# Moving one 32-byte tile so that the matmul operands of both layers start at 0 modulo 256 bytes

## The chip, the cores and the metric

The kernel runs as one program on one core of a Trainium2 chip. The metric is the device time of one execution in microseconds (us), lower is better. Engines are named as in the profile: PE is the matrix engine (PEld its loads of the stationary operand), DVE, ACT and POOL are the vector, scalar and GpSimd engines, SP issues most of the DMAs.

## The reference: what is computed

Two layers of a diffusion transformer on 256 image tokens and 256 context tokens, model width 2048, branch width 4096, all in float32. Cut to what matters:

```python
# layer 0: Fourier mixing, for x and for the context
u, z = split(h @ w_in)                        # h: 256 x 2048, w_in: 2048 x 8192
f = real(fft2(u, groups of 256)) ; f = einsum(f, w_mix)
x = x + gate * ((f * silu(z)) @ w_out[0])     # 4096 x 2048
# layer 1: attention, 64 query heads of 64, 8 key/value heads, window 128 plus the context
q, k, v, z = split(h @ w_in)                  # 2048 x 9216
o = softmax_with_sink(q k^T + mask) v
x = x + gate * ((o * silu(z)) @ w_out[1])
return rmsnorm(x, final_g)
```

In front of each layer stands `h = rmsnorm(x) * (1 + scale) + shift`, where shift, scale and gate come from a small product of the conditioning vector with 2048 x 6144 weights.

## The kernel before, in words

Every large product is done three times in a 32-bit format (`float32r`): both operands are split into a rounded high part and the rest, and PE adds high x high, high x low and low x high. The helper `mm3` (its three `PE.matmul` calls are lines 78 to 80 of the profile) does this. In `PE.matmul(o, stationary, moving)` the second argument is the stationary operand, which PEld loads (128 columns), and the third one is the moving operand, which streams through (up to 512 columns). While a matmul streams, PEld loads the stationary operand of the next.

```python
def mm3(o, wh, wl, xh, xl, start, stop):
    PE.matmul(o, wh, xh, start=start, stop=False)
    PE.matmul(o, wh, xl, start=False, stop=False)
    return PE.matmul(o, wl, xh, start=False, stop=stop).ins
```

Weights come in by DMA into `raw` tiles (128 x 2048, 3 buffers), and `half_split` cuts each into two halves of 1024 columns: ACT rounds one into `wh` (line 65), DVE subtracts to get `wl` (line 66). Activations lie in `act` tiles (128 x 512) in layer 0.

The stages, in the order of the program:
- Opening and Fourier part (to about 322 us): conditioning, a discrete Fourier transform over tokens, the product with the first half of `w_in`. Stationary operands are slices of 127 columns of the tiles `wmh`, `wml`, `wph`, `wpl`; the moving one is an `act` tile, 256 or 260 columns at a time.
- z and output products of layer 0 (322 to 1028 us): the stationary operand is 128 columns of `wh` or `wl`, the moving one a whole `act` tile of 512 columns. These are the groups `ps<-act,wh` and `ps<-act,wl`, 1024 matmuls for each of the lines 78 to 80. A group's name gives what is written, then the moving and then the stationary operand.
- k and v products of layer 1 (1028 to 1122 us): here the roles are swapped. The stationary operand is 128 columns of `h1` or `h1c` (the layer's input, high part in columns 0 to 255 and rest in 256 to 511), the moving one 512 columns of `wh` or `wl`: groups `ps<-wh,h`, `ps<-wl,h`, `ps<-wh,h1c` and so on, 384 matmuls.
- q products (768 matmuls of the same form with `h1`), z products (`ps<-h,wh` of line 1119 with 512 moving columns of `h1`, `ps<-h,wl` of line 1121 with 256) and attention, interleaved by hand (1122 to 1640 us). A loop over 64 heads does `stage_s` (scores: four matmuls `kkh` and `kkl` against `qa` or `qb`, lines 1155 and 1156, then maximum and exponential on DVE and ACT), one filler unit of a projection, `stage_o` of two heads earlier (eight float16 matmuls of lines 1190 and 1191) and another filler unit. A filler unit of q or of the output product is 12 matmuls. The first ten units run ahead of the loop.
- Output product of layer 1 (partly as filler, then 1640 to 1800 us): the moving operand is again `wh` or `wl`; the stationary one, 128 columns of `yh[k]`, lies for k = 0 to 15 in the buffers of the `h1` pool, for k = 16 to 23 in `act` tiles, for k = 24 to 31 in the pool `fin`.

The tile that the change moves is `dsc` (128 x 8 float32, 32 bytes in each partition): eight columns of scale factors, which `emit_y` reads as a per-partition scalar. It was allocated from the pool `h1`, ahead of that pool's 16 large buffers.

Pools are laid out one behind the other in each partition's memory, so the size of one sets the start of the next. `const` (the constants) comes first, then `raw`, `ws` (with `wh`, `wl`, `xh`), `act`, and behind them the pools of the stages. No scheduler's table and no queue is touched by the change.

Of the kernel before, what the change touches and what calls it, by code (L numbers as in the profile page):

```python
# [10 lines left out]
F32 = mybir.dt.float32  # L11
# [6 lines left out]
P = 128  # L18
# [13 lines left out]
def tile_dit(ctx: ExitStack, tc: tile.TileContext, a: dict, out: bass.AP):  # L32
# [3 lines left out]
    const = ctx.enter_context(tc.tile_pool(name="const", bufs=1))  # L36
# [66 lines left out]
    GP.memset(ones, 1.0)  # L103
    mhalf, pow_end = const.tile([P, 4], F32, name="mhalf"), [None]
    GP.memset(mhalf, -0.5)

    def bcast_rows(r4, dst):
        o = psum()
        for t in range(4):
            PE.matmul(o[:, t * P : (t + 1) * P], r4[:, t : t + 1].broadcast_to([P, P]), ident, start=True, stop=True)  # L110
        S.copy(dst, o)
# [775 lines left out]
    with tc.tile_pool(name="h1", reuse_waits="tile", bufs=16) as h1p:  # L887
        hx1 = []
        v01, vs = [], []
        dsc = h1p.tile([P, 8], F32, name="dsc", bufs=1)  # L890
        kT = []
        with tc.tile_pool(name="kvp", reuse_waits="tile", bufs=2) as kvp:
            hc1 = []
# [561 lines left out]
```

## Time and profile before

| what | value |
|---|---|
| time, median of 3 runs | 1803.8 us |
| the 3 runs | 1804.04, 1803.8, 1799.57 us |
| profiled execution: span of its instructions | 1799.6 us |
| profiled execution: its own time | 1799.6 us, nothing around the span counts; it agrees with the third run |
| PE busy | 1765.1 us, 98% of the span |
| PEld busy | 1478.0 us, 82% |
| DVE busy | 1411.3 us, 78% |
| ACT busy | 898.3 us, 50% |
| DMA | 398.86 MB, mean 222 GB/s |

The profiled execution is thus as quick as the quickest of the three runs, 4.2 us under their median. Two things matter in reading the page. Matmuls are pipelined: the duration of one in a record is longer than the distance from its start to the next one's start, so a chain of matmuls is timed by the distance of starts. And a view that counts the instructions in a stretch also counts those that straddle its ends, which makes a count of matmuls up to two too high.

### The profile page before, as it was taken

The numbers are of one execution on the slowest core, as the hardware profiler recorded it, in microseconds if no ns is written. First come the engines' busy times: TensorE is split into PE (matmuls) and PEld (weight loads), VectorE is DVE, ScalarE is ACT, GpSimd is POOL, SyncE is SP. The second block draws the span as 40 slices with busy tenths as digits, with TensorE's granted clock in tenths as the row PEclk, the third lists the DMA queues.
The fourth block names the chain that finished last, engine by engine and source line by source line (L and its number), as shares of the span: only waits on it lengthen the run. The fifth ranks groups of instructions, "written<-read, shape, count | busy, mean of one in ns | idle before, by whom it ended". The sixth has DMA issues, their size and how long they took to land. (4 is left out here: it accounts for less than half of the span.)

```text
span 1799.6 us, 26039 instructions
## 1 busy us (share of the span) xinstructions
PE 1765.1 (98%) x9449; PEld 1478.0 (82%) x9449; DVE 1411.3 (78%) x2761; ACT 898.3 (50%) x1543; POOL 213.5 (12%) x213
## 2 busy tenths in 40 slices
PE   6999999999999999999999999999999999999998
PEld 4679999888888888888888888878888788887886
DVE  5779888786978888775976563989999899997455
ACT  5545445432222242323322443678887788886343
POOL 0001112100000000000001000332212212233001
PEclk9999999999999999999999999999999999999999
DMA  9998889666666757663558322488888988888553
GB/s 393 417 341 230 236 228 249 230 227 241 239 229 234 260 194 264 245 223 117 189 203 336 120 104 94 168 189 217 213 209 204 211 209 209 211 211 263 192 176 140
DMA packets 205248, 398.86 MB, mean 222 GB/s; under 512 B 152064, under 2 KB 152464, under 8 KB 170048
## 3 DMA queue, kind: packets, MB, share of 16 engines
q1 hardware_dynamic: 181056, 359.19, 61.7%
q0 software_dynamic: 19920, 31.06, 6.7%
q10 hardware_dynamic: 4144, 6.95, 1.2%
q8 instruction: 74, 1.21, 0.3%
q14 instruction: 54, 0.44, 0.1%
HBM read 352.06 MB, written 12.59 MB: 203 GB/s over the span
## 5 line engine op out<-in xcount | busy, mean ns | idle before, releaser
L65 ACT CAST wh<-raw 128x1024 fp32r<-128x1024 f32 x333 | 348.3, 1048 | 532.4 <-PE ps L79 431.6
L66 DVE TENSOR_TENSOR wl<-raw,wh 128x1024 fp32r<-128x1024 f32 x333 | 428.0, 1289 | 219.1 <-ACT wh L65 215.4
L79 PE MATMUL ps<-act,wh 128*128 128x512 f32 x1024 | 398.2, 389 | 0.0
L78 PE MATMUL ps<-act,wh 128*128 128x512 f32 x1024 | 393.7, 389 | 0.0
L80 PE MATMUL ps<-act,wl 128*128 128x512 f32 x1024 | 392.8, 389 | 0.0
L80 PEld LDWEIGHTS ps<-act,wl 128*128 128x128 f32 x1024 | 192.2, 188 | 39.9
L79 PEld LDWEIGHTS ps<-act,wh 128*128 128x128 f32 x1024 | 192.2, 188 | 39.8
L78 PEld LDWEIGHTS ps<-act,wh 128*128 128x128 f32 x1024 | 192.2, 188 | 39.7
L1119 PE MATMUL ps<-h,wh 128*128 128x512 f32 x512 | 184.8, 396 | 0.0
L686 DVE CUSTOM_DVE_ANT_0 raw<-raw,cb 128x512 f32<-128x512 f32 x256 | 172.7, 689 | 12.7 <-DMA raw<-in_adw 8.9
L686 DVE CUSTOM_DVE_ANT_0 junk<-raw,cb 128x512 f32<-128x512 f32 x192 | 132.1, 688 | 31.0 <-DMA raw<-in_adw 20.4
L1121 PE MATMUL ps<-h,wl 128*128 128x256 f32 x512 | 138.6, 281 | 0.0
L79 PE MATMUL ps<-wl,h 128*128 128x512 f32 x320 | 126.9, 397 | 0.3 <-DVE wl L66 0.3
L80 PE MATMUL ps<-wh,h 128*128 128x512 f32 x320 | 125.3, 395 | 0.0
L78 PE MATMUL ps<-wh,h 128*128 128x512 f32 x320 | 124.0, 402 | 0.0
L1173 DVE SCALAR_TENSOR_TENSOR f<-p,sm,f 128x512 f16<-128x512 f32 x128 | 105.6, 844 | 11.1 <-ACT f L1172 10.9
L1119 PEld LDWEIGHTS ps<-h,wh 128*128 128x128 f32 x512 | 96.2, 188 | 18.9
L1160 ACT ACTIVATE p<-ps,mx 128x512 f32<-128x512 f32 x128 | 88.0, 689 | 36.9 <-DVE mx L1157 30.8
L1172 ACT ACTIVATE f<-p,sm 128x512 f16<-128x512 f32 x128 | 87.6, 717 | 33.6 <-DMA ft<-f 15.5
L1121 PEld LDWEIGHTS ps<-h,wl 128*128 128x128 f32 x512 | 96.6, 189 | 2.8
L1157 DVE CUSTOM_DVE_ANT_0 ps<-ps,mask,nsink 128x512 f32<-128x512 f32 x128 | 93.5, 750 | 0.9 <-PE ps L1156 0.7
L79 PE MATMUL ps<-wl,ys 128*128 128x512 f32 (+1 forms) x192 | 75.2, 392 | 0.0
(339 smaller groups left out, 3379.3 us busy)
## 6 DMA issues: line engine op xcount, KB each, us to landing
raw<-in_wz SPq DMA_DIRECT2D x64, 1024.0 KB, 5.4
raw<-in_adw SPq DMA_DIRECT2D x64, 1024.0 KB, 5.2
raw<-in_awp SPq DMA_DIRECT2D x32, 1024.0 KB, 13.0
raw<-in_wo SPq DMA_DIRECT2D x32, 1024.0 KB, 5.5
raw<-in_wq SPq DMA_DIRECT2D x32, 1024.0 KB, 5.3
raw<-in_wu SPq DMA_DIRECT2D x32, 1016.0 KB, 6.1
raw<-in_wo1b SPq DMA_DIRECT2D x16, 1024.0 KB, 4.9
act<-in_xT POOLq DMA_DIRECT2D x32, 256.0 KB, 6.0
```

The costliest lines, as they stand in the source:

```text
L65: last_cast[0] = S.copy(h, src).ins
L66: last_sub[0] = eng.tensor_tensor(l, src, h.bitcast(F32), op=ALU.subtract).ins
L78: PE.matmul(o, wh, xh, start=start, stop=False)
L79: PE.matmul(o, wh, xl, start=False, stop=False)
L80: return PE.matmul(o, wl, xh, start=False, stop=stop).ins
L686: V.tensor_tensor_reduce(junk if s == 0 and i < 3 else wf, wf, cb[:, s, kq * 512 : kq * 512 + 512], 1.0, 0.0, ALU.mult, ALU.add, acc[:, i, ...
L1119: PE.matmul(o[0], wh[:, q], hx1[k], start=k == 0, stop=k == KT - 1)
L1121: PE.matmul(o[0][:, 0:N], wl[:, q], hx1[k][:, 0:N], start=False, stop=False)
L1157: V.tensor_tensor_reduce(o, o, mask[:, tb, :], -0.125, nsink[:, i : i + 1], ALU.add, ALU.min, mx[:, tb : tb + 1])
L1160: S.activation(pt[tb], so[tb], AF.Exp, bias=mx[:, tb : tb + 1], scale=-1.0, accum_out=sm[:, tb : tb + 1])
L1172: S.activation(f[:, 0:512], pt[tb], AF.Copy, scale=sm[:, tb : tb + 1])
L1173: V.scalar_tensor_tensor(f[:, 512:1024], pt[tb], sm[:, tb : tb + 1], f[:, 0:512], op0=ALU.mult, op1=ALU.subtract)
```

## The change

`dsc` is allocated from `const`, right behind `mhalf`, and no longer from the pool `h1`.

```diff
     mhalf, pow_end = const.tile([P, 4], F32, name="mhalf"), [None]
     GP.memset(mhalf, -0.5)
+    dsc = const.tile([P, 8], F32, name="dsc")
...
     with tc.tile_pool(name="h1", reuse_waits="tile", bufs=16) as h1p:
         hx1 = []
         v01, vs = [], []
-        dsc = h1p.tile([P, 8], F32, name="dsc", bufs=1)
         kT = []
```

`const` grows by 32 bytes, so all that is laid out behind it moves up by 32 bytes, as far as the pool `h1`: that pool loses the 32 bytes in front of its buffers, which therefore stay where they were, and so does everything behind them. Start addresses in a partition, in bytes, from the two built programs:

| tiles | before | after | modulo 256 before | after |
|---|---|---|---|---|
| `raw` | 19680 + n x 8192 | 19712 + n x 8192 | 224 | 0 |
| `wh`, `wl`, `xh`, `xl` | 44256 + n x 4096 | 44288 + n x 4096 | 224 | 0 |
| `act` | 68832 + n x 2048 | 68864 + n x 2048 | 224 | 0 |
| `h1`, `yh` 0 to 15 | 142080 + n x 2048 | the same | 0 | 0 |
| `h1c` | 175360 + n x 2048 | the same | 0 | 0 |
| `kkh`, `kkl`, `qa`, `qb` | from 174848, 178944, 183040, 189184 | the same | 0 | 0 |
| `yh` 24 to 31 (pool `fin`) | 832 modulo 2048 | the same | 64 | 64 |
| `dh`, `dl` (token transform) | 185632, 189728 | the same | 32 | 32 |
| Fourier tiles (`wmh`, `aph`, `pqh`, ...) | various | all 32 higher | various | various |

A slice of a stationary operand (128 columns of float32) is 512 bytes on from the last, so it keeps the remainder; only the Fourier slices of 127 columns run through all multiples of 4.

On all five engines the two programs hold the same instructions in the same order, with the same waits; only addresses differ. Lines behind the new one are numbered one higher, and the same again behind the removed one.

## The prediction

> **What bounds the kernel now.** I read the page first (its busy shares), then the groups of matmuls by line and form, then stretches of the span with their counts, and last single starts in the timeline.
>
> ```profile
> PE 1765.1 (98%) x9449; PEld 1478.0 (82%) x9449; DVE 1411.3 (78%) x2761; ACT 898.3 (50%) x1543; POOL 213.5 (12%) x213
> PEclk9999999999999999999999999999999999999999
> ```
>
> PE is busy for 98% of the span at full granted clock. No clock is to be won, so the time moves only with what one matmul takes or with how long PE stands. The groups show that one shape, 128 stationary columns against 512 moving ones, has two durations (out, then moving and stationary operand; count, then busy us and mean ns of one):
>
> ```profile
> L80 PE MATMUL ps<-act,wl 128*128 128x512 f32 x1024 | 392.8, 389 | 0.0
> L79 PE MATMUL ps<-wl,h 128*128 128x512 f32 x320 | 126.9, 397 | 0.3 <-DVE wl L66 0.3
> L80 PE MATMUL ps<-wh,h1c 128*128 128x512 f32 x64 | 24.7, 396 | 0.0
> L79 PE MATMUL ps<-wl,ys 128*128 128x512 f32 x184 | 73.0, 397 | 0.0
> L79 PE MATMUL ps<-wl,act 128*128 128x512 f32 x56 | 21.8, 390 | 0.0
> ```
>
> Row one is layer 0: both operands at 224 modulo 256 bytes, 389 ns. Rows two to four are layer 1: moving operand at 224, stationary one at 0 (in `ys` partly 64), 396 to 397 ns. Row five is the control inside layer 1: the same moving `wl`, but the stationary operand lies in `act`, at 224 again, and it takes 390 ns. So it isn't the stage; it goes with where the two operands lie to each other. What counts for the time is the distance of starts, which a stretch of back-to-back matmuls gives:
>
> ```profile
> core 0: us, PE busy (x), PEclk, DMA share, GB/s
> 330.00:700.00 370.00, 370.00 (x1635) 1.00 0.63 230
> 1032.00:1117.00 85.00, 85.00 (x365) 1.00 0.30 104
> 1657.00:1701.00 44.00, 44.00 (x190) 1.00 0.54 192
> 1702.00:1723.00 21.00, 21.00 (x94) 1.00 0.58 201
> ```
>
> With two straddlers taken off: 370 / 1633 = 226.6 ns in layer 0; 85 / 363 = 234 and 44 / 188 = 234 ns with the stationary operand at 0. The last two rows are one loop, the output product of layer 1; only at about 1701 us does the stationary operand go from the `h1` buffers to `act`, and 21 us then hold 94, less two 228, less one 226 ns. In the timeline:
>
> ```profile
> 599.81 0.39 PE L79 MATMUL ps<-act,wh 128*128 128x512 f32 x1
> ...
> 600.49 0.39 PE L79 MATMUL ps<-act,wh 128*128 128x512 f32 x1
> ...
> 1278.40 0.39 PE L79 MATMUL ps<-wl,h 128*128 128x512 f32 x1
> ...
> 1279.79 0.40 PE L79 MATMUL ps<-wl,h 128*128 128x512 f32 x1
> ```
>
> Three matmuls in 0.68 us, 226.7 ns each, against six in 1.39 us, 231.7 ns. I take 226.7 and 233.2: the second is the mean of the stretches and of the filler units, and 6.5 ns the difference.
>
> **The change part by part.**
>
> *Layer 0, no term.* All of `wh`, `wl`, `xh`, `act` and the Fourier tiles move by the same 32 bytes, so no pair changes its relation. I take 0 for 3072 matmuls. What speaks for it is that a pair with both at 0 can be seen, the scores of attention:
>
> ```profile
> 1272.17 0.40 PE L78 MATMUL ps<-wh,h 128*128 128x512 f32 x1
> ...
> 1272.87 0.40 PE L1155 MATMUL ps<-kkh,qa 128*128 128x512 f32 x1
> 1273.10 0.39 PE L1156 MATMUL ps<-kkl,qa 128*128 128x512 f32 x1
> 1273.33 0.39 PE L1155 MATMUL ps<-kkh,qa 128*128 128x512 f32 x1
> 1273.55 0.39 PE L1156 MATMUL ps<-kkl,qa 128*128 128x512 f32 x1
> ```
>
> The three q matmuls ahead (224 against 0) take 0.70 us; three scores (0 against 0) take 0.68, as in layer 0. Not every head looks like this, though:
>
> ```profile
> L1155 PE MATMUL ps<-kkh,qa 128*128 128x512 f32 x64 | 25.4, 397 | 0.0
> L1156 PE MATMUL ps<-kkl,qa 128*128 128x512 f32 x64 | 25.0, 391 | 0.0
> ```
>
> By these means (397 and 391, against 389) a pair at 0 costs 2 to 8 ns more, with waits in line 1155. But these chains are four long, and a chain at 224 against 224 starts slowly too:
>
> ```profile
> 1630.76 0.39 PE L79 MATMUL ps<-wl,act 128*128 128x512 f32 x1
> ...
> 1632.61 0.40 PE L79 MATMUL ps<-wl,act 128*128 128x512 f32 x1
> ```
>
> Eight matmuls behind float16 ones take 1.85 us, 231 ns each, before a chain settles. So I read the means of the scores as unsettled chains. The ends for layer 0: a gain or loss of 3 ns each, 9 us both ways, if the settled distance at 0 is another.
>
> *Layer 1 outside attention.* The moving `wh` and `wl` come to 0, against `h1` and `h1c` at 0. By the loops: 384 matmuls of k and v, 120 of q ahead of the heads, and 288 in the last stage (k = 0 to 15, less the 96 that are filler), together 792, at 6.5 ns 5.1 us. PE stands nowhere there that matters, so all of it shortens the span. The 180 with `yh` 24 to 31 go from 224 against 64 to 0 against 64, a relation that no row shows: between minus and plus 6.5 ns, 1.2 us both ways; taken at 0.
>
> *Layer 1 inside attention.* 648 of q and 96 of the output product, in units of 12. A unit behind the scores would follow on a settled chain (6.5 ns); one behind the float16 matmuls has to settle first. From 231 for the first eight and 226.7 then, against 233.2, that is about 2.9 ns. Half and half, 4.7 ns: 3.5 us. The 256 scores themselves then no longer follow on an unsettled chain: 3 ns, 0.8 us (from 391 against 389 and the excess of 397, less its waits). The z products, 512 pairs:
>
> ```profile
> L1119 PE MATMUL ps<-h,wh 128*128 128x512 f32 x512 | 184.8, 396 | 0.0
> L1121 PE MATMUL ps<-h,wl 128*128 128x256 f32 x512 | 138.6, 281 | 0.0
> 1253.64 0.39 PE L1119 MATMUL ps<-h,wh 128*128 128x512 f32 x1
> ```
>
> They go from 0 against 224 to 0 against 0. Mean 396 with waits in it, yet single ones take 0.39, so they are nearer to the fast kind: between minus 2 and plus 6.5 ns; I take 2, 1.0 us. Together 5.3 us of PE time. Not all of it is span:
>
> ```profile
> 1160.00:1640.00 480.00, 473.14 (x2605) 392.07 (x2603) 446.91 (x826) 394.35 (x783) 123.92 (x99) 1.00 0.85 207
> PE ps L1190 <- DMA ft<-f: 4.7, 4, 2.1
> ```
>
> DVE (the third figure) works 447 of these 480 us, 93%. With 5 us less it would be at 94%, so PE stays the longer one; but PE already waits 4.7 us for `ft`, which hangs on DVE and ACT, and that wait is what comes late next. I count three quarters, 4.0 us; the ends are 2 and 5.3.
>
> *The opening.* `raw` is also where the weights land. The first 90 us are full of DMA:
>
> ```profile
> 0.00:90.00 90.00, 73.42 (x557) 51.09 (x558) 55.39 (x150) 48.95 (x82) 3.84 (x13) 1.00 0.99 405
> gbc<-gated POOLq DMA_DIRECT2D x1, 1024.0 KB, 7.4
> raw<-in_wo1b SPq DMA_DIRECT2D x16, 1024.0 KB, 4.9
> ```
>
> A load of the same size that already lands at 0 (`gbc`) is no quicker than one into `raw` at 224 (7.4 against 4.9 us, though on another queue), so I take 0, with 0 to 2 us as ends. The Trainium skill, "DMA: Bandwidth & Descriptors", "How a descriptor splits into AXI transactions", says that a descriptor not starting at a multiple of 256 bytes needs one transaction more; by its figures a row of 8192 bytes would go from 264 to 256 beats, an estimate of 3% of the opening's loads into `raw`. No run here shows that for SBUF writes.
>
> *The moved tile itself.* `dsc` is read as a scalar operand by the same 32 instructions; no instruction, wait or queue entry is added, removed or moved. Zero; what hides it is that DVE isn't on the end-setting path there.
>
> The sum: 5.1 + 4.0 = 9.1 us. From the profiled execution's 1799.6 us that is 1790.5; it lies 4.2 us under the median of the runs, from which it is 1803.8 - 9.1 = 1794.7 us, 0.50% less.
>
> **The rivals.**
>
> *Slower: the stationary operand's own place decides.* All slow rows have it at 0 or 64 and all settled fast ones at 224, so "224 is the good place" fits the long stretches as well. Then layer 0 falls to the slow kind: 3072 x 6.5 = 20.0 us more, layer 1 gains nothing, 1823.8 us. It decides from 9.1 / 3072 = 3.0 ns per matmul of layer 0 on. Against it stand the scores at 1272.87 us, settled with the stationary operand at 0. Chance 0.12.
>
> *No change: the distances don't come from the addresses,* or nothing of the gain reaches the end. Time 1803.8 us. The control rows (390 against 397 in one stage) speak against it, and the tail, where no engine but PE is close. Chance 0.10. The Trainium skill, "TensorE: Matmul & The Clock Gate", "Step-by-step: what each phase is for", is on this side: PE has two independent SBUF read ports, and loading the next weights takes no bandwidth from the running matmul. By it all those chains should have one distance; the trace disagrees (226.6 against 234 ns).
>
> *Faster by the loads too:* the opening's DMA gets quicker by up to 2 us on top, 1792.7 us. Chance 0.04, by the `gbc` row.
>
> **How the numbers follow.** The forecast, relation decides and layer 0 stays, has 0.74; its own range is 1789 to 1800 us: the attention part between 2 and 5.3, the two unknown relations by 1.2 and by 1 to 2, and a spread of runs of about 2 us. 0.3% of this kernel is 5.4 us, about what its measurement can tell from no change; runs here differ by 4.5. Of the forecast's share 0.12 falls within 0.3%, the rest is faster: with the loads 0.66 faster. Within 0.3%: 0.12 + 0.09 of no change + a weak form of the first rival (1 to 4 ns in layer 0) 0.02, so 0.23. Slower 0.11. The range goes from 1787 us (the sum, the upper ends of the attention part and of the loads, and the runs' spread) to 1806 (no change and the runs' spread); the first rival lies outside, as does a gain of 3 ns in layer 0.
>
> **What would show it.** Right: in 1032 to 1117 us about 377 matmuls where 365 stood, groups `ps<-wl,h`, `ps<-wh,h1c` at 389 to 391 ns, layer 0 still at 389 and 1635 in 370 us, `ps<-wl,ys` between 390 and 397 for its part at 64. Wrong: layer 0 at 392 or more (first rival); layer 1 still at 396 (second); or layer 1 at 390 and the stretch of the heads as long as before, with the waits for `ft` grown by as much.

## The result, and the profile after

The changed kernel took 1797.65 us (median of 8 runs, 1796.45 to 1800.93), the kernel before beside it 1803.69 us (8 runs, 1799.57 to 1804.44). The ratio is 0.9973, 95% interval [0.9963, 0.9982]: 6.0 us less by the medians. In a later comparison it was 1797.87 against 1802.33 us, ratio 0.9966 [0.9951, 0.9982]. The profiled execution after has a span of 1795.5 us against 1799.6 before, only 4.1 us less. Every other run here with both figures on record took 1.7 to 1.9 us longer than its span, so the profiled execution of before would stand at about 1801.4 us (an estimate), 2.3 us under its median, and not be the run of 1799.57 us, as the table ahead of the prediction reads it. That of after, 1797.29 us, lies 0.4 under its own median, so the two spans show less of the gain than the medians do.

The page, and then the same four stretches of the span that the prediction showed (us; PE busy us and number of matmuls; granted clock; DMA share; GB/s):

```profile
PE 1760.7 (98%) x9449; PEld 1479.2 (82%) x9449; DVE 1411.9 (79%) x2761; ACT 897.8 (50%) x1543; POOL 211.5 (12%) x213
```

```profile
330.00:700.00 370.00, 370.00 (x1634) 1.00 0.62 230
1032.00:1117.00 85.00, 85.00 (x376) 1.00 0.31 111
1657.00:1701.00 44.00, 44.00 (x196) 1.00 0.55 194
1702.00:1723.00 21.00, 21.00 (x94) 1.00 0.56 191
```

Layer 0 holds 1634 matmuls in 370 us where it held 1635, so it is where it was. The k and v products hold 376 in 85 us instead of 365, the output product 196 in 44 us instead of 190. The fourth row, where the stationary operand lies in `act`, had 94 and has 94. With the straddlers off, 85 / 374 = 227 ns: layer 1 now goes at the pace of layer 0.

The groups by line and form (count, then busy us and mean ns of one):

```profile
L80 PE MATMUL ps<-act,wl 128*128 128x512 f32 x1024 | 392.8, 389 | 0.0
L1119 PE MATMUL ps<-h,wh 128*128 128x512 f32 x512 | 187.4, 403 | 0.0
L1121 PE MATMUL ps<-h,wl 128*128 128x256 f32 x512 | 138.7, 281 | 0.0
L79 PE MATMUL ps<-wl,h 128*128 128x512 f32 x320 | 125.2, 391 | 0.9 <-DVE wl L66 0.9
L79 PE MATMUL ps<-wl,ys 128*128 128x512 f32 x184 | 72.3, 393 | 0.0
L1155 PE MATMUL ps<-kkh,qa 128*128 128x512 f32 x64 | 25.3, 395 | 0.0
L80 PE MATMUL ps<-wh,h1c 128*128 128x512 f32 x64 | 24.2, 389 | 0.0
```

`ps<-wl,h` fell from 397 to 391 and `ps<-wh,h1c` from 396 to 389, as forecast. `ps<-wl,ys`, part of which stays unequal (0 against 64), stopped at 393. One row went the wrong way: the z product of line 1119 rose from 396 to 403 ns.

Where the 4.1 us between the two profiles lie follows from the start times of the same matmul in both traces (us):

| stretch, from one matmul's start to the next one's | before | after | difference |
|---|---|---|---|
| start to first z matmul of layer 0 (opening, Fourier) | 322.3 | 321.1 | -1.2 |
| z and output products of layer 0 | 696.9 | 696.9 | 0.0 |
| row sums to first k, v matmul | 9.3 | 9.3 | 0.0 |
| k and v products | 89.7 | 87.2 | -2.5 |
| q ahead of the heads | 42.0 | 41.0 | -1.0 |
| attention (first score to last `ft,v` matmul) | 480.8 | 483.0 | +2.2 |
| output product after it | 149.3 | 147.6 | -1.7 |

Outside attention 6.4 us came in, in attention 2.2 were lost again; the remaining 0.1 is rounding. About 1.6 of the 2.2 us, by an estimate, is a stretch at half the granted clock that this execution has in attention and that of before has not (shown in the last section). The stretch 1160 to 1640 us (PE, PEld, DVE, ACT, POOL, clock, DMA) and PE's waits there:

```profile
1160.00:1640.00 480.00, 471.10 (x2599) 390.97 (x2598) 443.88 (x818) 391.32 (x778) 123.96 (x102) 1.00 0.86 210
```

```profile
PE ps L1190 <- ACT f L1172: 3.6, 3, 2.2
PE ps L1190 <- DMA ft<-f: 1.7, 3, 0.8
PE ps L1190 <- DVE ft L1183: 1.7, 1, 1.7
PE ps L1182 <- DVE f L1173: 1.1, 1, 1.1
PE ps L79 <- DVE wl L66: 0.9, 3, 0.5
```

The four rows for `f` and `ft` sum to 8.1 us (before 6.7). 1.7 of them is a wait at the end of the heads (`ft` L1183; 0.9 before, behind 1640 us) that comes and goes: it is 1.7 in the kernel below whose gain is undone (`pad_h1`), and 0.9 in one that keeps the gain (`fin_at_0`).

### The profile page after: what moved, and what is told of

Its sections match the earlier page's. It is cut to its first block, busy times and chain, and to the rows that moved or that the text cites. A ratio compares the mean times of both kernels' runs of the same rounds, so it can differ in the third digit from the quotient of the medians.

```text
span 1795.5 us, 26039 instructions
## 1 busy us (share of the span) xinstructions
PE 1760.7 (98%) x9449; PEld 1479.2 (82%) x9449; DVE 1411.9 (79%) x2761; ACT 897.8 (50%) x1543; POOL 211.5 (12%) x213
## 5 line engine op out<-in xcount | busy, mean ns | idle before, releaser
L79 PE MATMUL ps<-act,wh 128*128 128x512 f32 x1024 | 398.2, 389 | 0.0
L78 PE MATMUL ps<-act,wh 128*128 128x512 f32 x1024 | 393.7, 389 | 0.0
L79 PEld LDWEIGHTS ps<-act,wh 128*128 128x128 f32 x1024 | 192.2, 188 | 39.8
L78 PEld LDWEIGHTS ps<-act,wh 128*128 128x128 f32 x1024 | 192.2, 188 | 39.8
L79 PE MATMUL ps<-wl,h 128*128 128x512 f32 x320 | 125.2, 391 | 0.9 <-DVE wl L66 0.9
L78 PE MATMUL ps<-wh,h 128*128 128x512 f32 x320 | 122.4, 397 | 0.0
L79 PE MATMUL ps<-wl,ys 128*128 128x512 f32 (+1 forms) x192 | 74.5, 388 | 0.0
```

## The experiments

Two theories were open after the result. *Relation:* the pace hangs on how the starts of the moving and the stationary operand stand to each other modulo 256 bytes. *Place:* it hangs on the stationary operand's own start; the unchanged layer 0 (224 before, 0 after) already speaks against that. And for the 3.5 us that did not arrive in attention: is PE time there no longer worth anything, or was less of it saved than forecast? Start distances below are means over all undisturbed matmuls of 512 columns that follow another one, from the trace's single starts; a pair is written moving, then stationary start, modulo 256 bytes.

**One pool moved back.** A 32-byte tile ahead of the `h1` pool; the weights stay at 0.

```diff
     with tc.tile_pool(name="h1", reuse_waits="tile", bufs=16) as h1p:
+        pad1 = h1p.tile([P, 8], F32, name="pad1", bufs=1)
+        GP.memset(pad1, 0.0)
```

> The changed kernel with 32 bytes more ahead of the buffers of layer 1's pool, so that wh, wl and act stay at 0 modulo 256 and h1, h1c, kkh, qa go to 32 (yh 24 to 31 to 96). Relation theory (what counts is the distance of the two operands modulo 256, not where they lie): layer 1 is as in the kernel before, projections back at 233 ns (groups wh,h at 395 to 397), z products back at 229.5 ns, 1803 us, 0.998 to 1.002 of the kernel before; layer 0 stays at 226.7. Place theory (a start at 0 modulo 256 is good or bad by itself): z products, whose stationary operand wh stays at 0, stay at 234 ns, and the scores, now both at 32, change.

Measured 1802.76 us (11 runs), ratio to before 0.9998 [0.9988, 1.0009]. The stretches of layer 0 and of k and v, and the group of the z product (its line is 1121 in this kernel):

```profile
330.00:700.00 370.00, 370.00 (x1634) 1.00 0.62 230
1032.00:1117.00 85.00, 85.00 (x366) 1.00 0.30 106
```

```profile
L1121 PE MATMUL ps<-h,wh 128*128 128x512 f32 x512 | 184.7, 396 | 0.0
```

366 matmuls instead of 376: the k and v products are slow again (233.3 ns, 0 against 32). The z product is quick again (396, distance 229.7 at 32 against 0, where it had 0 against 224 before). Moving less stationary start is minus 32 in the one, as it was at 224 against 0, and plus 32 in the other, as it was at 0 against 224: both pace and difference are those of before, though each stationary operand lies somewhere else than it did. The place theory falls. Layer 0, which the edit leaves alone, keeps its 1634.

**The other pool moved.** The same pad between `ws` and `act`: layer 0's moving operands at 32, its weights at 0.

```diff
+    padp = ctx.enter_context(tc.tile_pool(name="pad", bufs=1))
+    pad0 = padp.tile([P, 8], F32, name="pad0")
+    nc.gpsimd.memset(pad0, 0.0)
     actp = ctx.enter_context(tc.tile_pool(name="act", bufs=33))
```

> The changed kernel with 32 bytes more ahead of the pool act: wh and wl stay at 0, act and all of layer 1's tiles go to 32. Relation theory: the 3067 matmuls of layer 0 lose their common start (moving 32 above stationary) and leave 226.7 ns for somewhere between 228 and 234: 4 to 22 us on top of the kernel before, 1808 to 1826 us, with the last stage's part on act tiles slow too; layer 1 as before. Place theory (the stationary operand's own start decides): layer 0's stationary wh stays at 0 as in the changed kernel, 226.7 ns, at most 1804 us.

Measured 1822.4 us (4 runs), ratio 1.0114 [1.0098, 1.0129].

```profile
330.00:700.00 370.00, 370.00 (x1588) 1.00 0.61 221
```

```profile
L83 PE MATMUL ps<-act,wl 128*128 128x512 f32 x1024 | 398.9, 395 | 0.0
```

1588 in place of 1634: 370 / 1586 = 233.3 ns. Layer 0's stage grew from 696.9 to 717.3 us, 20.4 us for 3072 matmuls, 6.6 ns each. A difference of plus 32 (32 against 0) costs in layer 0 what minus 32 (224 against 0) cost in layer 1.

**The z weights elsewhere.** In the z product the 512- and the 256-column matmul alternate. The weights get a column offset (0 as the control, 56, 8 or 32 float32 columns), so that they lie at 0, 224, 32 or 128; six constants of layer 0 move to another pool for the room.

```diff
-        h = wsp.tile([P, 1024], F32R, tag="ws", name="wh")
-        l = wsp.tile([P, 1024], F32R, tag="ws", name="wl")
+        h = wsp.tile([P, 1088], F32R, tag="ws", name="wh")[:, off : off + 1024]
+        l = wsp.tile([P, 1088], F32R, tag="ws", name="wl")[:, off : off + 1024]
...
-                return half_split(raws1[src], i % 2)
+                return half_split(raws1[src], i % 2, 56 if kind == "z" else 0)
```

> Control for the next: buffers of wh and wl are 256 bytes longer each (1088 columns, of which 1024 are used from column 0), and the room comes from moving five small layer-0 constants (1536 bytes) into the pool of layer 0; all starts modulo 256 as in the changed kernel. Both theories: as the changed kernel, 1796 to 1800 us, z products at 234.4 and 117.3 ns.

> As the control, but the z products' wh and wl use columns 56 to 1079, so that as stationary operands they start at 224 modulo 256, as before the change, while k, v, q and output products keep 0 against 0. Both theories: z products back from 234.4 to 229.5 and from 117.3 to 118.1 ns, 2.1 us less of PE's work in the attention stretch. If PE bounds that stretch: 2 us quicker than the control, ratio to it 0.9988, 1795.5 us. If DVE, ACT and the transposes bound it: not quicker, 1797.6 us, and PE's waits for ft and f grow by 2 us.

> The z weights at 32 modulo 256 bytes, their moving operand at 0, a pair that no run has shown in these chains. If the difference of the two starts modulo 256 decides, this is the relation of the slow projections (moving 224, stationary 0, 233.3 ns), seen in the z chains: the product of 512 columns takes more than the 229.3 ns of 0 against 224, and the pair with the 256-column one more than 347.2 ns. If only being alike or not counts, it is 229.3 and 118 ns as at 224.

> The z weights at 128 modulo 256 bytes, half a period from their moving operand. If the difference decides smoothly, the pair of 512 and 256 columns takes between the 347.2 ns of 0 against 224 and the 351.7 ns of 0 against 0, or as at 32. If only being alike or not counts, 347.2 ns.

Groups of line 1119 at 0, 224, 32 and 128, in this order:

```profile
L1119 PE MATMUL ps<-h,wh 128*128 128x512 f32 x512 | 186.5, 401 | 0.0
```

```profile
L1119 PE MATMUL ps<-h,wh 128*128 128x512 f32 x512 | 184.9, 397 | 0.0
```

```profile
L1119 PE MATMUL ps<-h,wh 128*128 128x512 f32 x512 | 186.9, 401 | 0.0
```

```profile
L1119 PE MATMUL ps<-h,wh 128*128 128x512 f32 x512 | 186.2, 399 | 0.0
```

| z weights at (moving at 0) | 512 columns, ns | 256 columns, ns | the pair |
|---|---|---|---|
| 0 | 234.4 | 117.2 | 351.6 |
| 224 | 229.5 | 118.2 | 347.7 |
| 32 | 233.6 | 118.1 | 351.7 |
| 128 | 231.5 | 119.4 | 350.9 |

Of the four, 224 is the best place and 0 with 32 the worst, each by one execution. So the sign and size of the difference count, not only whether it is zero, and this chain wants another difference than the projections. Why it does is open: here a load of the stationary operand (188 to 189 ns by the profile) outlasts the matmul of 256 columns that it runs beside (118 ns), which it doesn't in the other chains (227 ns), but no run tests that. But the time doesn't follow: 1797.18 us at 0 (5 runs, ratio 0.9966 [0.9954, 0.9979]), 1797.33 at 224 (11 runs, 0.9970 [0.9961, 0.9979]); the single executions at 32 and 128 gave 1796.21 and 1799.37. At 224 the z matmuls together took 512 x (351.6 - 347.7) ns = 2.0 us less than at 0, the attention 482.5 us against 481.3. But the 482.5 holds a stretch at half clock of about 1.6 us, and the 481.3 none: that execution has it behind attention. So the two profiles can't tell whether part of the 2.0 us arrived, and the whole times show nothing of it.

**The loads' place alone.** The moved tile goes behind `raw`, so `raw` is at 224 again and every matmul operand stays as changed.

```diff
     rawp = ctx.enter_context(tc.tile_pool(name="raw", bufs=3))
+    padp = ctx.enter_context(tc.tile_pool(name="pad", bufs=1))
...
-    dsc = const.tile([P, 8], F32, name="dsc")
+    dsc = padp.tile([P, 8], F32, name="dsc")
```

> The changed kernel with one difference: the 32-byte tile lies behind the raw buffers instead of in the constants, so the raw buffers, where the weights land, are at 224 modulo 256 bytes again and every matmul operand is where the change put it. If the place where the loads land is worth something, the layer-0 output product starts at about 322.3 us of the span (322.3 before, 321.1 after), the 8192-byte packets of the opening take 313 ns instead of 309, and the whole is about 1.2 us longer than the changed kernel, 1798.8 us. If the 1.2 us came from the Fourier matmuls' own operands, or by chance, the product starts at 321.1 us and the time is that of the changed kernel, 1797.6 us.

The first z matmul of layer 0 in the timeline, before, after and in this kernel (where one line more makes L79 of L78):

```profile
322.28 0.39 PE L78 MATMUL ps<-act,wh 128*128 128x512 f32 x1
```

```profile
321.12 0.39 PE L78 MATMUL ps<-act,wh 128*128 128x512 f32 x1
```

```profile
322.43 0.39 PE L79 MATMUL ps<-act,wh 128*128 128x512 f32 x1
```

The first 90 us, after (first row) and here (second row):

```profile
0.00:90.00 90.00, 74.71 (x566) 52.38 (x570) 55.32 (x150) 49.08 (x83) 3.82 (x13) 1.00 0.99 410
```

```profile
0.00:90.00 90.00, 73.21 (x556) 51.26 (x557) 55.32 (x150) 49.07 (x82) 3.81 (x13) 1.00 0.99 406
```

With `raw` at 224 the opening moves 406 GB/s (405 before) and the stage ends at 322.4 us; at 0 it moves 410 and ends at 321.1. The median packet of 8192 bytes between 30 and 60 us took 313 ns in both kernels with `raw` at 224 and 309 ns in both executions of the changed kernel. All other profiles with `raw` at 0 had this start at 320.6 to 321.1 us, but for one at 321.8 (the kernel with z matmuls added, below), which stays open. So the step belongs to the loads' place. The whole time was 1797.86 us (11 runs, 1794.11 to 1802.69), on another chip than the changed kernel's second comparison; the kernel before took 1800.76 us there. The ratio, 0.9982 [0.9971, 0.9993], lies 1.6 to 2.9 us above the 0.9973 and 0.9966 of the changed kernel, the way that was expected, but the intervals overlap.

**The last stationary buffers.** `yh` 24 to 31 from 64 to 0.

```diff
-            ss = fp.tile([P, 9], F32, name="ss")
+            ss = fp.tile([P, 64], F32, name="ss")
```

> The changed kernel with the tile ahead of the last eight stationary buffers widened from 9 to 64 columns, so these eight lie at 0 modulo 256 bytes instead of 64. If the relation of the two starts decides, the 181 matmuls at 0 against 64 (233.2 ns) fall to about 227, 1.1 us less, all of it behind the attention: about 1796.5 us. If 64 is near enough to 0, or their pace comes from something else, they stay at 233.2 and the time is 1797.6 us.

15 us of the last stretch, after (first row) and here (second row, 5 us earlier as the end is):

```profile
1770.00:1785.00 15.00, 15.00 (x72) 1.00 0.12 43
```

```profile
1765.00:1780.00 15.00, 15.00 (x74) 1.00 0.12 43
```

The 181 matmuls fell from 233.2 to 226.7 ns, and the output product after attention from 147.6 to 146.5 us: minus 64 costs as much as 32 either way. The time was 1793.02 us (5 runs, 1792.14 to 1797.18; before beside it 1800.76), ratio 0.9964 [0.9950, 0.9978]. It is the lowest time here, but on the chip where the kernel before is also quicker, and the ratio is that of the changed kernel (0.9966 and 0.9973) within its interval: the 1.1 us are shown by the stage, not by the whole time. The profiled execution also had the shortest attention of all, 479.3 us, in which this edit changes nothing of the pairs and no stretch at half clock lies.

**Both small edits** (z weights at 224, last buffers at 0):

> Both small edits on the changed kernel: the z weights at 224 modulo 256 bytes against their moving operand at 0 (the quicker place, 2.6 us of TensorE time by the run with that edit alone), and the last eight stationary buffers at 0. If the attention is set by other engines, only the second edit arrives: about 1796.3 us. If both arrive, 1793.9 us.

1796.23 us (11 runs), ratio 0.9976 [0.9967, 0.9985]; output product after attention 146.5 us, attention 481.3. The second edit shows in its stage; of the first nothing can be seen in the time.

**Less and more work in attention.** 64 of the 512 low-part z matmuls left out, and the same 64 done twice.

```diff
-                            else:
+                            elif k % 8 != 3:
                                 PE.matmul(o[0][:, 0:N], wl[:, q], hx1[k][:, 0:N], start=False, stop=False)
```

```diff
                                 PE.matmul(o[0][:, 0:N], wl[:, q], hx1[k][:, 0:N], start=False, stop=False)
+                                if k % 8 == 3:
+                                    PE.matmul(o[0][:, 0:N], wl[:, q], hx1[k][:, 0:N], start=False, stop=False)
```

> The changed kernel without 64 of the 512 low-part z matmuls of 256 columns (each eighth k step), so part of the z product is not computed. At 117.3 ns each that is 7.5 us of TensorE time inside the attention. If TensorE sets the attention's length, the stretch from the first score to the last ft,v matmul falls from 483.0 to 475.5 us and the time to about 1790.1 us. If the transposed tiles ft and with them VectorE and ScalarE set it, the stretch stays within 1 us of 481 to 483, the waits of TensorE for ft and f grow by about 7 us, and the time is 1796 to 1798 us. In between, the share of 7.5 us that arrives is the share that any saving of TensorE time in this stage is worth.

> The changed kernel with 64 low-part z matmuls of 256 columns done a second time (the same eight of each 64 that were left out before), so a part of the z product is added twice. That is 7.5 us more TensorE time inside the attention. Leaving 7.5 us out made that stage 9 us longer, with 11 us more waits for ft. If the stage is a balance of TensorE and of the chain that makes ft, with TensorE the longer one on this side, the stage grows by 7 to 9 us to about 491 us, the waits for ft stay or shrink, and the time is about 1805 us. If the chain for ft sets the length and the run without the matmuls was slower only by the way the waits fell, the added work fills waits: the stage stays within 3 us of 483 and the time is 1797 to 1801 us.

PE's waits in attention, with less (three rows) and with more (three rows):

```profile
PE ps L1190 <- DMA ft<-f: 18.1, 16, 5.4
PE ps L1190 <- ACT f L1172: 2.2, 1, 2.2
...
PE ps L79 <- DVE wl L66: 0.6, 2, 0.4
```

```profile
PE ps L1192 <- DMA ft<-f: 5.2, 6, 2.1
PE ps L1192 <- ACT f L1174: 2.1, 1, 2.1
PE ps L1192 <- DVE ft L1185: 1.2, 2, 0.8
```

With 7.5 us less the attention was 491.9 us long and the time 1804.47 us (11 runs, ratio 1.0022 [1.0013, 1.0031]), longer than with them; with 7.5 us more it was 488.2 and 1801.04 us (12 runs, 0.9987 [0.9974, 0.9999]). Neither was expected as it came. The pair is not the clean test it was meant to be: in both built programs, units around the z products stand in another order than in the changed kernel (in the first, the eight `ft,v` matmuls of one head stand behind a z unit instead of inside it). What they show is that the length of this stage hangs on when `ft` comes, whose waits went to 18 us with PE less busy; two stretches at half clock (last section) lie in that execution's attention as well. How much a pure change of PE's work would be worth they don't show.

**The changed kernel again**, beside the kernel before:

> The changed kernel itself, again, beside the kernel before on the same chip. If its gain is that of the first comparison, it is about 6 us, a ratio of 0.9967 to 0.9975. It also settles what the runs with the raw buffers at 224 and with the last stationary buffers at 0 are to be compared with: if the stage gains of the profiles are real, the changed kernel lies 1 us under the first and 1 us over the second.

1797.87 us (10 runs), ratio 0.9966 [0.9951, 0.9982]: the gain is there again, 4.5 us by the medians. The second part of the expectation can't be read from the medians, since the kernels with `raw` at 224 and with the last buffers at 0 ran on another chip. By the ratios, each to the kernel before on its own chip, the first lies 2.9 us over this one and the second 0.4 us under it, where 1 and 1 were expected; the intervals cover both.

**What the attention made of it.** All kernels here but those with less and more work issue the same matmuls there in the same order. The sums of start distances of the q, output, score and z matmuls, each counted without what it waited, and the stage's length (us):

| operands in attention | sum of those matmuls | attention, each profile | mean |
|---|---|---|---|
| as before (before, and the two with a pad) | 403.4 | 480.8, 483.8, 481.6 | 482.1 |
| as after (five profiles) | 401.7 | 483.0, 482.2, 482.4, 481.3, 479.3 | 481.6 |
| z weights at 224 (two profiles) | 400.2 | 482.5, 481.3 | 481.9 |

3.2 us of matmul time went, and the stage's mean changed by 0.2 to 0.5 us, while single profiles of one group differ by up to 3.7. Part of that spread has a name: a stretch at half clock (last section), about 1.6 us, lies in the attention of the profiles with 481.6, 483.0, 482.2, 482.4 and 482.5 us, and partly in the one with 483.8; none lies in the others. The plus 2.2 us between the two profiles of the result is thus mostly such a stretch, and the rest lies within the spread. How much of the saved matmul time arrives in this stage stays open.

## Why the prediction was right, and where its sum was off

1794.7 us was forecast, and 1797.65 measured, inside the range; the gain has the forecast mechanism and two thirds of its size (6.0 of 9.1 us; in the second comparison half, 4.5). By the ratio it is 0.27%, which falls within 0.3% (forecast chance 0.23), by the medians 0.33%, which falls in faster (0.66): it lies at the edge of the two. That the total came so near owes 1.2 us to the opening, which the sum had at nothing. By steps:

- *Layer 0, no term:* right. 696.9 us before and after, 226.7 ns both at 224 and at 0. With that row the rival (the stationary operand's own place) fell, and again in the first experiment.
- *Layer 1 outside attention, 5.1 us:* right. The three stages gave 2.5 + 1.0 + 1.7 = 5.2 us. (The trace has 161 q matmuls ahead of the first score where the sum counted 120; that moves 0.3 us from the next step to this one.) The 180 (181 in the trace) with `yh` 24 to 31 were taken at no change, and 0 against 64 had 233.2 ns, as 224 against 64 had 234.1: right within 0.2 us.
- *Layer 1 inside attention, 4.0 us:* this is the step that failed. Of its 5.3 us of PE time the q and output units gave 3.2 (3.5 forecast, though by its own figures a unit behind float16 matmuls gains 3.6 ns a matmul and not 2.9, which makes 3.8), the scores 0.4 (0.8), and the z products, forecast to gain 1.0, lost 2.0, some 4 ns a pair, outside the ends that were given (minus 2 to plus 6.5). The step took 0 against 0 to be the quick pair for every chain, from the projections and the scores. For the alternating chain of 512 and 256 columns 0 against 224, which it had, is the quickest of the four pairs tried. So 1.7 us was saved, not 5.3. And of that three quarters were to arrive: by the table above it was 0.5 us, with a spread that doesn't exclude all or nothing. The z weights at 224 don't settle it either (1.5 us less work, 0.3 us longer by the means, with the spread above). The wait for `ft` the prediction had named as what comes late next; whether it counted it too low is argued, not shown.
- *The opening, 0 (ends 0 and 2 us):* mis-sized; it gave 1.2 to 1.3 us. The reading that misled was the comparison of `gbc` with `raw`, loads on two queues: it can't show 1%. The Trainium skill, "DMA: Bandwidth & Descriptors", "How a descriptor splits into AXI transactions", had the right sign here: the prediction's estimate from it, 3% for a row of 8192 bytes (by that section's way of counting, 263 beats against 256 and not 264, an estimate of 2.7%), compares with 313 to 309 ns, 1.3%, and 406 to 410 GB/s, 1.0%.
- *The moved tile itself:* right; no stage shows a price for it.

The sum of what was measured outside attention, 1.2 + 5.2 = 6.4 us, with an attention that stands within its spread, agrees with the 6.0 and 4.5 us of the two comparisons.

## What to carry to other kernels

When two groups of the same matmul shape differ by 2% in one kernel, compare the starts of both operands modulo 256 bytes: one small tile in the wrong pool can set all pools behind it off, and here cost 6.5 ns on each matmul of the projections that follow one another. Back-to-back matmuls of one width want equal starts, but try the pair for each kind of chain, since an alternating one wanted another. And count a saving in full only in stages where nothing but TensorE is near its limit: outside attention all of it arrived here (5.2 of 5.1 us forecast), but where results of a long chain through other engines are already waited for, 1.7 us of saved matmul time could not be found again in the stage's length.

## What the runs showed of the hardware that was not expected

- The pace of matmuls that follow one another hangs on where their two operands start: 226.7 ns for 512 columns at equal starts modulo 256 bytes (both 224, or both 0), 233.2 to 233.3 at differences of 32 either way and at minus 64. A difference of 128 was tried in the z chain alone. That the load of the next stationary operand disturbs the running stream would explain it; no run here shows it apart. The Trainium skill, "TensorE: Matmul & The Clock Gate", "Step-by-step: what each phase is for", gives the array two independent read ports for the two operands; taken as no disturbance, the traces here disagree with it by 6.5 ns in 227, 2.9%.
- The place where a load lands costs too: 1% of the opening's transfer rate (406 against 410 GB/s), 1.2 us of this kernel.
- After a wait of 2.2 us TensorE ran at half its clock for 3.4 us in some executions. The profile after shows it in attention (us; PE busy us and count; granted clock; DMA share; GB/s). That of the control with the z weights at 0 (second fence) doesn't show it there, but later, behind attention. The profile before (third fence) has the same wait, 2.1 us, and stays at full clock:

```profile
1165.00:1168.40 3.40, 1.20 (x10) 1.00 1.02 197
1168.50:1171.50 3.00, 3.00 (x11) 0.52 1.02 322
1171.60:1175.00 3.40, 3.40 (x20) 0.94 0.42 78
```

```profile
1168.50:1171.50 3.00, 3.00 (x19) 1.00 1.03 315
1637.00:1640.00 3.00, 3.00 (x10) 0.53 1.02 430
```

```profile
1168.70:1172.10 3.40, 1.58 (x7) 1.00 1.01 181
1172.10:1175.10 3.00, 2.76 (x18) 1.00 0.84 313
```

11 matmuls stand where 19 do at full clock. It costs about 1.6 us: in the control, where it lies in the output product, that stage takes 149.3 us instead of 147.7. The Trainium skill, "TensorE: Matmul & The Clock Gate", "What's actually happening", speaks of half the clock after at least one idle window of about 3.4 us; here 2.2 us of wait within 3.4 us that were two thirds idle were enough, though not each time. What tells the cases apart can be read from the traces' records of the granted clock. Within a trace they change only at whole multiples of 3.41 us from one another, and each stretch at half clock between 330 us and the last matmul lasts 3.41 us. PE was busy for at most 41% of the 3.41 us ahead of each of these 12 stretches (35% in the first fence), and for at least 43% of every such 3.41 us that full clock followed (46% in the third fence). So the same wait costs something or nothing by how it falls on these steps, which lie elsewhere in each execution. That fits all 14 profiles here; no run set it on purpose.
